# A hybrid decoder on one core: the first layer's W1 product in two column chunks as seven half-size products, x kept in memory meanwhile

## The chip, the cores and the metric

The kernel runs on one core of one Trainium2 chip. The metric is the time of one execution in device microseconds (us), the median of several runs; less is better. Engine names: PE is the matrix engine, DVE the vector engine, ACT the scalar engine, POOL the GpSimd engine, SP the engine that issues most transfers.

## What is computed

Two decoder layers on a sequence of 512 tokens with 1024 channels, everything in 32-bit floats. Each layer has a mixer (a windowed-mean mixer in the first layer, a gated spatial mixer, "SGU", in the second) and then an MLP; both are modulated by columns computed from a conditioning vector.

```
c_act = silu(c)
for i in range(2):
    sh1, sc1, g1, sh2, sc2, g2 = split(c_act @ ada_w[i] + ada_b[i], 6)
    h = rmsnorm(x, norm_mix_g[i]) * (1 + sc1) + sh1
    x = x + g1 * mixer_i(h)
    h = rmsnorm(x, norm_mlp_g[i]) * (1 + sc2) + sh2
    x = x + g2 * (square(relu(h @ mlp_w1[i])) @ mlp_w2[i])     # 1024 -> 4096 -> 1024
return rmsnorm(x, final_g)
```

## The kernel before

**Precision.** A 32-bit product is made from rounded parts. Each operand is split into a high part (a rounding copy on ACT, line 169 for weights, 594 for activations) and the rest (a subtraction on DVE, lines 170 and 595), and `mm3` (lines 176 to 182) issues three matmuls for one product: low by high, high by low, high by high. One split covers a weight block of 128 x 1024 in a buffer pair `wh`, `wl`; there are five such pairs.

**The MLP** is `mlp(i, ...)`, called once for each layer. The 4096 hidden columns come in four chunks of 1024. M1 is the product with W1, which gives one chunk of hidden values `g`; M2 multiplies a chunk by its 1024 rows of W2 and adds into `y`. The work is a list of units, written out by hand, which PE runs in that order:

- `f` units (`f_run`): an M1 product for 128 hidden columns, all 1024 input channels and all 512 tokens: 24 matmuls of width 512 in the first layer (`n = 256 if i else S`), 48 of width 256 in the second.
- `s` units (`s_run`): the seven half-size products of Strassen's scheme in Winograd's form for M1, for 512 hidden columns (a "quad" `(c, j)`): each has 24 matmuls of width 256. Seven `s` units do what four `f` units do. Their token-side sums (`as`, `sums_a`) are made once by `a_sums`; their weight-side sums are made in `s_prep`: two by a DVE addition (line 708), two by an accumulating transfer on POOL's queue (line 703).
- `p` units (`p_run`): the same scheme for M2 of chunks 0 to 2, seven units a chunk, 24 matmuls of width 512 each. `by_dma` (line 757) says how the weight-side sums are made. In the second layer POOL issues accumulating transfers of 1 MB into the tile `bt` (`b_add`, line 767): after the split for product 1 the block for product 5 is added, then the one for 6, then for 4, in this chain, and one more sum into a tile `b`. In the first layer DVE adds blocks that were loaded plainly (lines 783, 790, 806, 814).
- `q` units (`q_run`): M2 of chunk 3 done plainly, with the gated update of x (`gated`, lines 967 to 969) behind each.

In the first layer M1 consists of `f` units alone: seven column blocks of chunk 0 are computed in the "sweep" while the normalised input `hb` is made (lines 545 to 571), then 25 `f` units, 24 of them spread between the `p` units of the chunk before. In the second layer only chunk 0 is `f` units; chunks 1 to 3 are `s` units, two to three between any two `p` units. For each unit a `prep` function loads and splits its weights; `ahead` lets it run some units before the unit itself.

**What else fits between.** The modulation columns (`ada_tile`: a load of 512 KB and a DVE multiply-and-sum, line 202) are 128 channels each; 56 of them are computed in this manner behind the start: in the first layer's MLP 32, one every 0.69 unit (`due`); in SGU 24 (16 in its `u` loop, 8 in its output loop). `spread_cols` turns eight finished columns into the row tile `gb` with which `gated` multiplies: a transpose on PE, a copy on ACT, two transfers on POOL's queue.

**Room.** The token-side sums of the `s` units need two tiles of 1 MB. In the second layer they lie where x lay: `spill` writes x to memory, `reload` brings it back after the last `s` unit.

## Time and profile before

| | |
|---|---|
| three runs, median (range) | 866.25 us (865.43 to 867.08) |
| the profiled execution: time, span from first to last instruction | 867.54 us, 865.5 us |
| PE busy, weight loads busy | 850.8 us, 734.4 us |
| DVE busy, ACT busy, POOL busy | 667.8 us, 447.8 us, 49.4 us |
| granted PE clock | 0.998 |
| moved by DMA | 163.39 MB, mean 189 GB/s |

Busy times are unions of instruction records. A matmul's record is longer than the distance to the next one, since matmuls are pipelined: the distance between starts is what PE's time goes by. Line numbers are those of the kernel before. A group line of the profile gives line, engine, operation, out<-in tiles, shapes, count, then busy time, mean ns of one, and the engine's idle time before it with what ended it. "core N" windows give busy us (count) of PE, weight loads, DVE, ACT and POOL, then the clock, the DMA engines' mean busy share and GB/s.

### The profile page before, as it was taken

The page shows a single profiled execution, that of the slowest core. Times are in us where ns is not written, and L with a number is a line of the kernel's source. Part 1 is how long each engine was busy: PE and PEld are TensorE (multiplying, and loading weights), DVE is VectorE, ACT ScalarE, POOL GpSimd, SP SyncE. Part 2 cuts the span into 40 slices and gives each one's busy share as a digit, 9 for nine tenths or more (in the row PEclk, how much of TensorE's full clock was granted, in tenths as well). Part 3 has the DMA queues.
Part 4 walks back from the last instruction along what each step waited for, and adds up shares of the span by engine and source line. Part 5 has one row for each costly group of instructions (what it writes and reads, how often), then busy time and mean ns, then how long its engine had stood idle before and what let it go on. Part 6 is the DMA issues. An engine that isn't in the chain of part 4 may idle for free. (4 is left out here: it accounts for less than half of the span.)

```text
span 865.5 us, 11809 instructions
## 1 busy us (share of the span) xinstructions
PE 850.8 (98%) x4592; PEld 734.4 (85%) x4592; DVE 667.8 (77%) x884; ACT 447.8 (52%) x653; POOL 49.4 (6%) x69
## 2 busy tenths in 40 slices
PE   8999999999999999999999999999999999999996
PEld 7778888888888888888888888999999988999885
DVE  6889797788869886657798866667787598779855
ACT  5285755454444445238332326656765576567521
POOL 3000000000000000000020001001101000100001
PEclk9999999999999999999999999999999999999999
DMA  9969855453455341606757525946778587778302
GB/s 352 417 226 320 292 177 195 164 183 138 178 206 170 122 171 49 219 25 219 245 172 243 192 73 205 333 95 149 195 226 183 150 204 229 160 162 262 127 24 98
DMA packets 40045, 163.39 MB, mean 189 GB/s; under 512 B 4507, under 2 KB 4659, under 8 KB 34742
## 3 DMA queue, kind: packets, MB, share of 16 engines
q1 hardware_dynamic: 35282, 137.72, 44.4%
q0 software_dynamic: 4560, 24.66, 13.7%
q8 instruction: 36, 0.59, 0.3%
q10 hardware_dynamic: 148, 0.27, 0.1%
q14 instruction: 19, 0.16, 0.1%
HBM read 158.42 MB, written 4.21 MB: 188 GB/s over the span
## 5 line engine op out<-in xcount | busy, mean ns | idle before, releaser
L179 PE MATMUL po<-hb,wl 128*128 128x256 f32 (+1 forms) x624 | 207.7, 333 | 1.2 <-DVE wl L170 1.2
L180 PE MATMUL po<-hb,wh 128*128 128x256 f32 (+1 forms) x624 | 206.9, 332 | 0.2 <-DVE hb L595 0.2
L182 PE MATMUL po<-hb,wh 128*128 128x256 f32 (+1 forms) x624 | 206.7, 331 | 0.0
L170 DVE TENSOR_TENSOR wl<-raw,wh 128x1024 fp32r<-128x1024 f32 (+1 forms) x110 | 130.8, 1192 | 43.9 <-ACT wh L169 43.6
L169 ACT ACTIVATE wh<-raw 128x1024 fp32r<-128x1024 f32 (+1 forms) x110 | 113.1, 1034 | 67.3 <-PE pm L182 29.5
L182 PE MATMUL pm<-wh,oh 128*128 128x512 f32 x356 | 130.9, 377 | 0.0
L180 PE MATMUL pm<-wl,oh 128*128 128x512 f32 x336 | 130.8, 389 | 0.0
L179 PE MATMUL pm<-wh,ol 128*128 128x512 f32 x336 | 130.8, 389 | 0.0
L179 PEld LDWEIGHTS po<-hb,wl 128*128 128x128 f32 x624 | 117.2, 188 | 14.1 <-DVE wl L170 2.1
L180 PEld LDWEIGHTS po<-hb,wh 128*128 128x128 f32 x624 | 117.2, 188 | 12.0 <-DVE hb L595 0.4
L182 PEld LDWEIGHTS po<-hb,wh 128*128 128x128 f32 x624 | 117.1, 188 | 11.8
L170 DVE TENSOR_TENSOR wl<-b,wh 128x1024 fp32r<-128x1024 f32 x60 | 72.7, 1220 | 22.1 <-ACT wh L169 21.9
L202 DVE SCALAR_TENSOR_TENSOR ada<-ada,cb 128x1024 f32<-128x1024 f32 x56 | 68.1, 1218 | 19.4 <-DMA ada<-in_ada 19.1
L182 PEld LDWEIGHTS pm<-wh,oh 128*128 128x128 f32 x356 | 66.9, 188 | 13.9
L180 PEld LDWEIGHTS pm<-wl,oh 128*128 128x128 f32 x336 | 63.1, 188 | 12.4
L179 PEld LDWEIGHTS pm<-wh,ol 128*128 128x128 f32 x336 | 63.1, 188 | 12.4
L169 ACT ACTIVATE wh<-b 128x1024 fp32r<-128x1024 f32 x60 | 63.1, 1055 | 10.0 <-PE pm L182 6.5
L632 ACT ACTIVATE g<-po 128x512 f32<-128x512 f32 x40 | 23.6, 599 | 80.5 <-PE po L182 78.5
L170 DVE TENSOR_TENSOR wl<-bt,wh 128x1024 fp32r<-128x1024 f32 x24 | 29.0, 1222 | 35.0 <-ACT wh L169 35.0
L973 ACT ACTIVATE tmp<-x 128x512 f32<-128x512 f32 (+1 forms) x25 | 15.3, 612 | 63.3 <-DVE x L969 63.3
L862 DVE TENSOR_TENSOR y<-y,pm 128x512 f32<-128x512 f32 x68 | 43.5, 679 | 0.0
L179 PE MATMUL po<-as,wl 128*128 128x256 f32 x144 | 40.0, 278 | 0.9 <-DVE wl L170 0.9
(211 smaller groups left out, 1459.3 us busy)
## 6 DMA issues: line engine op xcount, KB each, us to landing
ada<-in_ada SPq DMA_DIRECT2D x72, 512.0 KB, 3.7
b<-in_w SPq DMA_DIRECT2D x21, 1024.0 KB, 5.2
raw<-in_w SPq DMA_DIRECT2D x25, 512.0 KB, 4.2
raw<-in_w1b SPq DMA_DIRECT2D x24, 512.0 KB, 6.3
bt<-in_w POOLq DMA_DIRECT2D x9, 1024.0 KB, 8.3
raw<-in_w2e SPq DMA_DIRECT2D x16, 512.0 KB, 3.2
raw<-in_w1b POOLq DMA_DIRECT2D x12, 512.0 KB, 5.4
wh<-in_ada SPq DMA_DIRECT2D x9, 512.0 KB, 9.6
```

Of the source, the lines that this page charges most:

```text
L169: A.activation(h[:, c], r[:, c], AF.Copy)
L170: V.tensor_tensor(l[:, c], r[:, c], f32(h[:, c]), ALU.subtract)
L179: T.matmul(o, wl, mh, start=first, stop=False, **kw)
L180: T.matmul(o, wh, ml, start=False, stop=False, **kw)
L182: T.matmul(o[:, c], wh, mh[:, c], start=False, stop=last and c.stop is None, **kw)
L202: V.scalar_tensor_tensor(r, r, 1.0, cb, ALU.mult, ALU.mult, accum_out=pmv[i, b][:, j : j + 1])
L632: A.activation(t, po, AF.Relu)
L862: V.tensor_tensor(yt, yt, banks[hf], ALU.subtract if minus else ALU.add)
L973: A.activation(tmp, xt, AF.Square, scale=D**-0.5, accum_out=s[:, len(cs) : len(cs) + 1])
```

## The change

- `FROM = (2, 1)`: the first layer's M1 for chunks 2 and 3 runs as 28 `s` units in place of 16 `f` units, in the order that the second layer has for chunks 1 to 3. W1's columns for them join the array `w1b`, indexed by `quad_at`.
- `a_parts` makes the token-side sums of the first layer from the split input (both parts subtracted, then added) in four steps, ahead of units 12, 13, 14 and 16.
- The first layer's nine remaining `f` units use width 256 too. The last matmul of a unit is cut in two (`narrow`, `two`) ahead of an `f` unit as well, and at the end of the sweep.
- x is written to memory from ACT's queue at the end of the sweep and brought back after the last `s` unit, as in the second layer.
- `by_dma = True`: the first layer's M2 sums too come from accumulating transfers on POOL's queue.
- The columns: 24 in the first layer's MLP at written-out units (`COLUMNS`: 12 of them at units 0 to 11, one at 18, 23, 28, 33, 38, 43 and 48 each into `gb`'s place, five at 58 to 61), 24 in SGU (19 in the `u` loop, 5 in the output loop), and 8 in the second layer's MLP, at units 8, 10, ... 22, into `gb`'s place. `spread_cols` for the MLP gains moves to unit 53 and to unit 30 of the second layer.
- `gb` is a tile of its own at each use; the input tile is placed anew ahead of the second layer's mixer.

```diff
+COLUMNS = (0, 1, 2, 3, 4, 5, 6, 7, 8, 9, 10, 11, 18, 23, 28, 33, 38, 43, 48, 58, 59, 60, 61, 61)
+A_PARTS = (12, 13, 14, 16)
...
+    def late_gb():
+        r = get_gb()
+        A.activation(r[:, 0:1], f32(latest[0])[:, 0:1], AF.Copy)
+        return r
...
+    def spill(h, queue=G):
+        xd.append(dram.tile([P, 2, D], F32, name=f"xd{h}{len(h32)}"))
+        queue.dma_start(xd[h], x_[h])
...
-                mm3(sweep[f], ((wh[:, fs[f]], wl[:, fs[f]])), (xh, xl), k == 0, k == KD - 1)
+                two = S // 2 if (k, f) == (KD - 1, SWEEP - 1) else None
+                mm3(sweep[f], ((wh[:, fs[f]], wl[:, fs[f]])), (xh, xl), k == 0, k == KD - 1, two)
+        for h in range(2):
+            spill(h, nc.scalar)
...
+    FROM = (2, 1)
...
-                n = 256 if i else S
+                n = 256
...
+            def a_parts(step):
+                blocks = [[H(slice(4 * j, 4 * j + 4), slice(256 * r, 256 * r + 256)) for j in range(2)] for r in range(2)]
...
+                def difference(p, q):
+                    t, u = scratch("s"), scratch("u")
+                    for n, o in enumerate((t, u)):
+                        V.tensor_tensor(o, f32(p[n]), f32(q[n]), ALU.subtract)
+                    V.tensor_tensor(t, t, u, ALU.add)
+                    return t
+                if step == 0:
+                    sums_a.update({1: blocks[0][0], 2: blocks[0][1], 4: blocks[1][1]})
+                    shift(hx, LINE - GAP)
+                    m, o = 5, operand(hx, "hx")
+                    sums_a["t"] = difference(blocks[1][0], blocks[1][1])
+                elif step < 3:
+                    m, o = (6, operand(big, "x0")) if step == 1 else (3, operand(big, "x1"))
+                    for q in range(2):
+                        V.tensor_tensor(sums_a["t"], sums_a["t"], f32(blocks[0][step - 1][q]), ALU.subtract if step == 1 else ALU.add)
+                else:
+                    m, o = 7, blocks[1][0]
+                    sums_a["t"] = difference(blocks[0][0], blocks[1][0])
+                parts(o, sums_a["t"] if step < 2 else sums_a.pop("t"))
+                sums_a[m] = o
...
-            by_dma = i == 1
+            by_dma = True
...
-                if i == 0:
+                if c + 1 < FROM[i]:
                     fs, lead, step = [("f", (c + 1, f)) for f in range(8)], 3, (1,) * 7
                 else:
                     fs, lead, step = [("s", (c + 1, j, m)) for j in range(2) for m in ORDER], 3, (2, 2, 2, 2, 2, 1, 0)
...
-                if i == 0:
+                if i == 0 and ("s", (FROM[0], 0, 1)) not in units[: n + 5]:
                     return min(n + 3, len(units))
...
+                if i == 0 and n in A_PARTS:
+                    a_parts(A_PARTS.index(n))
-                narrow[:] = [units[n + 1 : n + 2] and (units[n + 1][0] == "s" or i and units[n + 1] == ("q", (1, NT - 1)))]
+                narrow[:] = [units[n + 1 : n + 2] and (units[n + 1][0] in "sf" or i and units[n + 1] == ("q", (1, NT - 1)))]
...
-                if i and u == (3, 1, 4):
+                if u == (3, 1, 4):
                     reload()
...
+    ex = [(n, modulation(q, get_gb if 12 <= q < 19 else get4)) for q, n in enumerate(COLUMNS)]
+    ex.insert(19, (53, lambda: spread_cols(mods[0][:, c_g(1, 0) : c_g(1, 0) + KD], "gain0")))
+    mlp(0, first0, ex, gated, ending0)
...
+    ex = [(8 + 2 * q, modulation(48 + q, late_gb if q == 0 else get_gb)) for q in range(8)]
+    ex += [(30, lambda: spread_cols(mods[1][:, c_g(1, 0) : c_g(1, 0) + KD], "gain1"))]
+    mlp(1, first1, ex, last1, lambda: None)
...
+    w1b = np.concatenate([w1[0][:, 2 * D :], w1[1][:, D:]], axis=1)
+    d["w1b"] = w1b.reshape(2, 4, P, 10, 2, 256).transpose(3, 0, 4, 2, 1, 5).reshape(10, 2, 2, P, D)
```

The unit numbers of the first layer after the change: 0 the last `f` of chunk 0; 1 to 15 the eight `f` units of chunk 1 and the seven `p` of chunk 0; 16 to 36 the 14 `s` of chunk 2 and the seven `p` of chunk 1; 37 to 57 the 14 `s` of chunk 3 and the seven `p` of chunk 2; 58 to 65 the `q` units. In the second layer 0 to 3 are `f` units, and 4 to 24, 25 to 45 and 46 to 66 hold 14 `s` and seven `p` each.

More of the change, by code (lines that the diff above doesn't have):

```diff
@@ L941, in mlp @@
             ready = {}
-            extra = list(extra)
-            due, at = max(0.4, len(extra) / max(1, len(units) - 6)), 0
+            extra, at = list(extra), 0
             for n, (kind, u) in enumerate(units):
@@ L954, in mlp @@
                     a_sums(u[1] - 4)
-                if i and (kind, u) == ("p", (0, 1)):
-                    spread_cols(gain, "gain1")
-                if i and u == (3, 1, 4):
+                if u == (3, 1, 4):
                     reload()
@@ L1022, in first0, with modulation, ending0 @@
         return SWEEP
-    ex = [lambda q=q: ada_tile(0, 40 + q, ada1[q], get4) for q in range(8)]
-    ex += [lambda q=q: ada_tile(1, q, ada1[8 + q], get4) for q in range(24)]
-    ex.insert(12, lambda: spread_cols(mods[0][:, c_g(1, 0) : c_g(1, 0) + KD], "gain0"))
-    mlp(0, first0, ex, gated, lambda: normed(0, 1, 0))
+    def modulation(q, get):
+        return lambda: ada_tile(0 if q < 8 else 1, 40 + q if q < 8 else q - 8, ada1[q], get)
+    def ending0():
+        h_[0] = hparts(0)
+        normed(0, 1, 0)
+    ex = [(n, modulation(q, get_gb if 12 <= q < 19 else get4)) for q, n in enumerate(COLUMNS)]
+    ex.insert(19, (53, lambda: spread_cols(mods[0][:, c_g(1, 0) : c_g(1, 0) + KD], "gain0")))
+    mlp(0, first0, ex, gated, ending0)
     def blocks(src):
@@ L1076, in decoder_kernel @@
         u, gt, wu = {}, {}, {}
-        ex = [lambda: spread_cols(mods[1][:, c_g(0, 0) : c_g(0, 0) + KD], "gainm")]
-        ex += [lambda q=q: ada_tile(1, q, ada1[8 + q], get4) for q in range(24, 40)]
+        ex = [modulation(q, get4) for q in range(24, 32)]
+        ex += [lambda: spread_cols(mods[1][:, c_g(0, 0) : c_g(0, 0) + KD], "gainm")]
+        ex += [modulation(q, get4) for q in range(32, 43)]
         def do_u(n):
@@ L1111, in decoder_kernel @@
             (do_u if op[0] == "u" else do_mix)(int(op[1]))
-        ex += [lambda q=q: ada_tile(1, 40 + q, ada1[48 + q], get4) for q in range(8)]
+        ex += [modulation(q, get4) for q in range(43, 48)]
         h_[0] = hparts(GAP)
```

44 lines of the change are left out of this document (26 added, 18 removed).

## The prediction

> **What bounds the kernel now.** I read the page first: how much of the span PE is busy, and how busy its helpers are beside it.
>
> ```profile
> span 865.5 us, 11809 instructions
> PE 850.8 (98%) x4592; PEld 734.4 (85%) x4592; DVE 667.8 (77%) x884; ACT 447.8 (52%) x653; POOL 49.4 (6%) x69
> DVE  6889797788869886657798866667787598779855
> ```
>
> PE is busy 98% of the span, so only fewer or cheaper matmuls, or waits, can move the time. DVE at 77% is the second engine. In the waits of PE, almost nothing stands behind the start-up:
>
> ```profile
> PE po L179 <- DVE wl L170: 2.1, 4, 0.9
> ```
>
> Four times, 2.1 us in all, PE waited for the low part of a weight block. Next, PE's timeline tells what a unit costs. First a first-layer `f` unit (the start of one and of the next), then the second layer's `s` units (the first one, the next one, one that came late, and the end of the whole stretch).
>
> ```profile
> 267.14 0.39 PE L179 MATMUL po<-hb,wl 128*128 128x512 f32 x1
> ...
> 272.58 0.39 PE L179 MATMUL po<-hb,wl 128*128 128x512 f32 x1
> ```
>
> ```profile
> 583.50 0.28 PE L179 MATMUL po<-hb,wl 128*128 128x256 f32 x1
> ...
> 586.22 0.28 PE L179 MATMUL po<-as,wl 128*128 128x256 f32 x1
> ...
> 591.65 0.39 PE L179 MATMUL pm<-wh,ol 128*128 128x512 f32 x1
> ...
> 668.21 0.39 PE L179 MATMUL pm<-wh,ol 128*128 128x512 f32 x1
> ...
> 699.27 0.36 PE L179 MATMUL po<-as,wl 128*128 128x256 f32 x1 [0.86 <-DVE wl L170]
> ...
> 745.89 0.39 PE L179 MATMUL pm<-wh,ol 128*128 128x512 f32 x1
> ...
> 814.14 0.39 PE L179 MATMUL pm<-wh,ql 128*128 128x512 f32 x1
> ```
>
> An `f` unit takes 272.58 - 267.14 = 5.44 us for 24 matmuls, 0.2267 each at width 512. An `s` unit takes 586.22 - 583.50 = 2.72 us for 24, 0.1133 each at width 256: exactly half. The second layer's 42 `s` and 21 `p` units (24 matmuls of width 512 each, so 5.44) should take 42 x 2.72 + 21 x 5.44 = 228.5 us; they took 814.14 - 583.50 = 230.6. So the new arrangement of the first layer already runs in this trace, in the second layer, and loses 2.1 us over three chunks, of which about 1.0 is the one wait at 699.27 and the rest, 0.05 per `p`, the alternation of widths.
>
> **Matmuls.** Sixteen `f` units go: 16 x 5.44 = 87.04 us. Twenty-eight `s` units come: 28 x 2.72 = 76.16. That is **-10.9 us**, and all of it is on the path, since PE is. The nine other `f` units keep their time (48 x 0.1133 = 24 x 0.2267). Alternation: 21 `p` units at 0.05, **+1.0**.
>
> A rule speaks against this. The Trainium skill (TensorE: Matmul & The Clock Gate, Back-to-back issue gap) says that matmul spacing is set by weight load and matmul together and gives 81 ns at width 128 and 131 at 512, so that halving the width does not halve the spacing; estimated by a straight line, 98 ns at 256, the 28 units would cost 65.9 us against 50.3 for the 16. The trace disagrees: 0.1133 against 0.2267.
>
> **Work of DVE.** It is not on the path now; does it stay off? The rows of its pieces, and two starts that follow each other directly:
>
> ```profile
> L202 DVE SCALAR_TENSOR_TENSOR ada<-ada,cb 128x1024 f32<-128x1024 f32 x56 | 68.1, 1218 | 19.4 <-DMA ada<-in_ada 19.1
> L708 DVE TENSOR_TENSOR raw<-raw 128x1024 f32<-128x1024 f32 x12 | 14.6, 1220 | 0.1
> L783 DVE TENSOR_TENSOR b<-b 128x2048 f32<-128x2048 f32 x3 | 6.9, 2284 | 0.0
> L814 DVE TENSOR_TENSOR b<-b 128x2048 f32<-128x2048 f32 x3 | 6.8, 2281 | 0.0
> L747 DVE TENSOR_TENSOR g<-g,po 128x512 f32<-128x512 f32 x6 | 4.1, 680 | 0.3 <-PE po L182 0.3
> ```
>
> ```profile
> 156.99 1.22 DVE L170 TENSOR_TENSOR wl<-raw,wh 128x1024 fp32r<-128x1024 f32 x1
> 158.13 1.27 DVE L862 TENSOR_TENSOR y<-y,pm 128x512 f32<-128x512 f32 x2
> ```
>
> A piece of 1.22 us lets the next one start after 1.14. Removed: the four M2 additions (lines 783 to 814, of which the first and last are shown) x three chunks x 2.28 = 27.4 us, and eight columns, about 1.3 each with their small followers, 10.4. Added: 14 pieces of `a_parts` (4, 3, 3 and 4) x 1.14 = 16.0; two weight sums for each of four quads (line 708), 9.1; three additions from PSUM for each quad (line 747 and its like), 12 x 0.6 = 7.2; 12 more splits, 13.7. Net +8 us over 220. That is little, but it isn't spread evenly. The windows hold the first layer's chunk 1 stage and the second layer's first two:
>
> ```profile
> 186.00:262.00 76.00, 76.00 (x338) 62.81 (x337) 61.69 (x71) 35.29 (x45) 1.28 (x2) 1.00 0.47 169
> 668.00:746.00 78.00, 77.14 (x516) 70.56 (x515) 61.63 (x64) 47.26 (x57) 6.81 (x8) 1.00 0.74 190
> 583.00:668.00 85.00, 85.00 (x589) 78.62 (x589) 65.77 (x62) 57.94 (x75) 8.79 (x11) 1.00 0.72 184
> ```
>
> The row 668 to 746 has the very units that the first layer will have as 16 to 36: DVE 61.6 us. There, the last step of `a_parts` (4 x 1.14 = 4.6) and four columns (5.2) come on top: 71.4 us in 7 x 5.44 + 14 x 2.72 = 76.2, or 94%. The first three steps of `a_parts` (11.4) lie at units 12 to 14, where the additions that go (two of 2.28 there) and lead make room; the sums are wanted only from unit 17 on, so I cost them at nothing, and at their full 11.4 if that room isn't there. In the second layer's first chunk the eight columns raise 65.8 to 76 of 85 us. ACT, at 47 of 78 us, has room.
>
> **The chain of accumulating transfers.** The sums for M2 products 1, 5, 6 form a chain: split, transfer, split, transfer, split. The first layer has no such chain now and gets three. POOL's timeline shows the first and third link of each of the second layer's three chains, and the line's own view the time to landing:
>
> ```profile
> 586.80 0.85 POOL L767 DMA_DIRECT2D bt<-in_w  x1 [9.97 <-DVE wl L170]
> ...
> 612.23 0.88 POOL L767 DMA_DIRECT2D bt<-in_w  x1 [2.76 <-DVE wl L170]
> ...
> 664.10 0.85 POOL L767 DMA_DIRECT2D bt<-in_w  x1 [2.02 <-DVE wl L170]
> ...
> 691.81 0.85 POOL L767 DMA_DIRECT2D bt<-in_w  x1 [13.26 <-DVE wl L170]
> ...
> 742.38 0.85 POOL L767 DMA_DIRECT2D bt<-in_w  x1 [2.62 <-DVE wl L170]
> ...
> 768.20 0.86 POOL L767 DMA_DIRECT2D bt<-in_w  x1 [13.04 <-DVE wl L170]
> ```
>
> ```profile
> DMA to landing us min/median/max: 7.8/8.4/9.8
> ```
>
> PE goes from product 1 to product 6 in 2 x (5.44 + 2 x 2.72) = 21.8 us. The chain took 25.4, 27.7 and 25.8: it slips by 3.7, 5.9 and 4.1. What it may slip is its lead, the first link's issue ahead of product 1 on PE (591.65, 668.21, 745.89): 4.9, 4.1 and 3.5. Only the second overran clearly (by 1.8), and it is the one with the wait at 699.27: while ACT and DVE stand at the split that needs the transfer, the splits of the `s` units queue behind it. So an overrun costs its size less about 0.7, and no chain has anything to spare. What I expect: first layer, chunk 0: the cover is the lead there (p1's split ends some 10 us early, below), so 0. Chunk 1: slip 4.6 (the mean) and one column, 1.3, is 5.9; a lead of 4.2 less some 1.3 for the crowded DVE is 2.9; 3.0 over, costs 2.3. Chunk 2: slip 5.9 with a column, lead 4.2, costs 1.0. Second layer, chunk 0, with three columns on the chain: slip 3.7 + 3.9, lead 4.9, costs 2.0 if all of them fall on it, 0 if they fill DVE's idle time; I take 1.0. Together **+4.3** (0 to 10).
>
> The Trainium skill (DMA: Bandwidth & Descriptors, Measured) has 6.15 us for a 1 MB transfer issued from GpSimd. By that, an estimate, each link would be over 2 us shorter, no chain would slip, and the sum would be lower by the whole 4.3. The trace's 8.4, for accumulating ones among other traffic, decides.
>
> **Writing x out.** Two transfers of 1 MB from ACT's queue, with nothing to wait for, start about 92 us, among the loads for the first units.
>
> ```profile
> 100.00:104.00 4.00, 4.00 (x19) 3.32 (x18) 1.20 (x2) 4.00 (x8) 0.00 (x0) 1.00 0.98 352
> ```
>
> ```profile
> 104.77 1.22 DVE L170 TENSOR_TENSOR wl<-raw,wh 128x1024 fp32r<-128x1024 f32 x1
> ```
>
> ```profile
> 114.67 0.39 PE L179 MATMUL po<-hb,wl 128*128 128x512 f32 x1
> ```
>
> The DMA engines are full there (0.98, 352 GB/s), so 2 MB delay the loads by 2.1/0.352 = 6 us. The split that ends at 106.0 is wanted at 114.67: 8.7 us of lead cover it. I cost it at nothing; twice the delay would cost 3. Bringing x back happens as in the second layer, where nothing waited.
>
> **SGU.** Three fewer columns in its output loop, three more in its `u` loop. At the end of that loop a column lies ahead of the input's low parts, and PE waits right after:
>
> ```profile
> 531.79 1.22 DVE L202 SCALAR_TENSOR_TENSOR ada<-ada,cb 128x1024 f32<-128x1024 f32 x1
> ```
>
> ```profile
> 535.89 0.38 PE L179 MATMUL po<-hb,wl 128*128 128x256 f32 x1 [0.22 <-DVE wl L170]
> ```
>
> Gone, it gives at most its 1.14 us; against a possible loss of as much in the `u` loop I take **-0.5** (-1.1 to +1.1). The moved `spread_cols` have two POOL transfers each, and whatever accumulating transfer is queued behind the second waits for the first to land. At unit 53 no such transfer follows but x's return; at unit 30 of the second layer the next in line is the sum for product 4, wanted 20 us later. Nothing.
>
> **Sum.** -10.9 + 1.0 + 4.3 - 0.5 = -6.1 us. The profiled execution took 867.5 (span 865.5 and 2.0 around it), so 861.4 for its like; it lies 1.3 above the median of 866.25, for which the sum gives **860.2**.
>
> **Rivals.** *DVE becomes the bound (slower).* In 668 to 746 DVE idles 78.0 - 61.6 = 16.4 us, partly because it stands in order behind ACT's wait for the transfers. If this idle time cannot be filled by the added 9.8 us, units 16 to 36 take 71.4 + 16.4 = 87.8 instead of 76.2: 11.6 lost there, and 1.0 each in the two other chains. -10.9 + 1.0 + 13.6 - 0.5 = +3.2: 869.5. It decides as soon as all waits together pass 10.4. For it: 94%, five buffer pairs, and the second layer lost only 1.0 at 79%. Against: columns and `a_parts` hang on no transfer and can lie in just that idle time.
>
> *The waits don't come.* The columns fill the gaps, the chains hold: -10.9 + 1.0 + 0 - 0.5 = -10.4: 855.9. For it: two of three chains lost nothing. Against: their lead is used up.
>
> *Half the width isn't half the time.* With the first layer's `s` units on the weight load instead (734.4/4592 = 0.160 us each by the page), they would take 28 x 24 x 0.160 = 107.5, +20.5 with the rest of the sum as it is: 891. Against: 0.1133 in the second layer, same operands, same shapes. The skill's rule above is this case.
>
> **How the numbers follow.** Forecast (waits between 1 and 8 us) 0.62; no waits 0.19; DVE the bound or waits above 8: 0.17; half width dear 0.02. A measurement of this kernel can tell about 0.2%, 1.7 us, from no change. Faster: the forecast, the second rival and none of the others, less a little at the upper edge, 0.80; waits of 8.7 to 12.1 are within 0.2%, 0.07; slower 0.13. The range goes from 855.5 (no waits) to 865.0 (waits of 9.1) and leaves out about 0.17, nearly all above.
>
> **What would show it.** Matmuls of width 256 on `as` and `hb` in the first layer at 0.1133 apart, and M1 and M2 there (units 0 to 57) shorter by 5 to 11 us: the first term. PE waits on "DVE wl" or on ACT behind `bt`, near products 5 and 6 of chunks 1 and 2 and in the second layer's first chunk: the third. DVE above 90% in units 16 to 36 with waits below 3 us would refute the first rival. I am wrong if PE's waits in the first layer sum to over 8 us, if the first units wait for loads that x's way out delays, or if the `s` units' spacing isn't 0.1133.

## The result and the profile after

| | median of the runs (range) | against before in the same job |
|---|---|---|
| before | 865.84 us (864.63 to 867.08) | |
| changed | 898.69 us (898.25 to 899.08) | 1.0379 times [1.0361, 1.0397] |

The forecast was 860.2, 855.5 to 865.0. The page of the changed kernel, the lines that answer to those of before:

```profile
span 896.5 us, 13013 instructions
PE 857.0 (96%) x5116; PEld 758.1 (85%) x5116; DVE 685.5 (76%) x918; ACT 467.8 (52%) x682; POOL 66.7 (7%) x91
DVE  6889466897898688677798856666788698779855
PEclk9999999998999999999999999999999999999999
```

PE is down from 98% to 96% of a longer span: it stood for 39.5 us where it stood for 14.7 before, 24.8 more. DVE is no busier by share than before. The tenth slice (202 to 224 us) shows a lower granted clock, which before had nowhere. To see where the time went, the run is cut at starts of matmuls. The first layer's M1 and M2 run from the first of these rows of PE's timeline to the second:

```profile
122.62 0.39 PE L186 MATMUL pm<-wh,ol 128*128 128x512 f32 x1
...
364.11 0.39 PE L186 MATMUL pm<-wh,ql 128*128 128x512 f32 x1
```

That is 241.5 us. The same cut in every profiled execution, in us ("layer 1" and "layer 2" are these M1/M2 stages; "q", the plain product for chunk 3, follows layer 1; "M1, chunk 0" is what lies between SGU and layer 2's first M2 product):

| kernel | start | layer 1 | q | SGU | M1, chunk 0 | layer 2 | end | span |
|---|---|---|---|---|---|---|---|---|
| before | 120.1 | 228.6 | 45.3 | 141.9 | 55.8 | 222.5 | 51.4 | 865.5 |
| changed | 122.6 | 241.5 | 45.3 | 146.8 | 55.8 | 232.8 | 51.6 | 896.5 |
| E1 no column transfers | 121.9 | 227.3 | 45.3 | 141.9 | 53.8 | 224.2 | 51.8 | 866.2 |
| E2 M2's sums by DVE | 121.2 | 230.1 | 45.7 | 147.1 | 53.6 | 233.9 | 51.6 | 883.2 |
| E3 x written out later | 122.6 | 242.3 | 45.7 | 144.6 | 56.0 | 234.3 | 51.7 | 897.0 |
| E4 before, M2's sums by transfers | 119.6 | 245.7 | 45.3 | 141.9 | 54.7 | 223.3 | 51.2 | 881.8 |
| E6 E4 without column transfers | 119.5 | 228.6 | 45.3 | 141.5 | 55.1 | 222.0 | 51.5 | 863.5 |
| E10 E1 without `a_parts`' sums | 121.8 | 223.2 | 45.3 | 142.2 | 53.6 | 223.5 | 51.9 | 861.6 |
| E11 eight columns moved to SGU | 121.3 | 245.6 | 46.0 | 143.7 | 54.2 | 222.2 | 51.9 | 884.8 |
| E13 columns paced, waited for | 121.2 | 244.4 | 45.8 | 144.7 | 53.6 | 234.9 | 51.7 | 896.2 |
| E18 columns paced, not waited for | 121.6 | 236.5 | 45.3 | 151.0 | 54.4 | 225.5 | 51.7 | 886.0 |

The 31 us are layer 1 (+12.9), layer 2 (+10.3), SGU (+4.9) and the start (+2.5). Most of the start's 2.5 is no wait: from 60 to 100 us the 512-wide matmuls follow each other at 0.233 us in the changed kernel and in every one built from it, at 0.227 in before, E4 and E6; 167 of them make 1.1 us. In the changed kernel the 194 of width 256 behind them are 0.1177 apart, not 0.1133, which makes another 0.9. No run tests the reason; that the place of buffers can do such a thing is seen in E17 below.

Layer 1 was to be 228.6 - 10.9 + 1.0 = 218.7 us without waits, so it lost 22.8. What PE waited for in it (columns: total us, times, longest):

```profile
PE po L186 <- DVE wl L177: 5.0, 4, 2.1
PE pm L187 <- DVE wl L177: 5.0, 2, 3.4
PE po L186 <- ACT g L810: 3.7, 1, 3.7
PE pm L186 <- DVE ol L621: 1.2, 1, 1.2
```

Together 14.9 us, where before has no PE wait in this stage. All lie before 230 us, while M2 works on chunk 0 and the first units of chunk 1, but for one of 0.26 us. They are mostly waits for low parts of weight blocks (`wl`, 10.0 us). What holds DVE up is in the groups of its instructions, here of the whole span; the row that answers to line 202 is

```profile
L209 DVE SCALAR_TENSOR_TENSOR ada<-ada,cb 128x1024 f32<-128x1024 f32 x56 | 68.3, 1221 | 53.7 <-DMA ada<-in_ada 53.4
```

The same 56 column instructions as before, as long as before, but DVE stood 53.4 us ahead of them for their transfers, not 19.1; in layer 1 it is 21.2 us, against 8.6. The columns' time from issue to landing between 100 and 345 us, before and then changed:

```profile
DMA to landing us min/median/max: 3.1/3.3/5.0
```

```profile
DMA to landing us min/median/max: 3.4/5.2/11.7
```

The longest such wait of DVE, in DVE's and ACT's timelines (start, duration, and in brackets the idle time before it and its releaser):

```profile
121.95 1.22 DVE L858 TENSOR_TENSOR s<-s,g 128x1024 f32<-128x1024 f32 x1
131.46 1.23 DVE L209 SCALAR_TENSOR_TENSOR ada<-ada,cb 128x1024 f32<-128x1024 f32 x1 [8.29 <-DMA ada<-in_ada]
132.61 0.08 DVE L209 DVE_READ_ACCUMULATOR ada<-ada,cb 128x1 f32 x1
132.61 1.22 DVE L177 TENSOR_TENSOR wl<-bt,wh 128x1024 fp32r<-128x1024 f32 x1
```

```profile
130.74 1.06 ACT L176 ACTIVATE wh<-bt 128x1024 fp32r<-128x1024 f32 x1 [10.62 <-DMA bt<-in_w]
```

For 8 us of chunk 0 DVE stands at a column and ACT at the tile of the chain, both for transfers that are under way together. The DMA view of 113 to 133 us shows what is on the way, with each queue's packets, MB and share of the 16 engines:

```profile
DMA packets 1076, 4.96 MB, mean 248 GB/s; under 512 B 128, under 2 KB 128, under 8 KB 818
q0 software_dynamic: 288, 2.10, 53.7%
q1 hardware_dynamic: 786, 2.83, 38.4%
ada<-in_ada SPq DMA_DIRECT2D x3, 512.0 KB, 11.2
b<-in_w POOLq DMA_DIRECT2D x1, 1024.0 KB, 10.4
bt<-in_w POOLq DMA_DIRECT2D x1, 1024.0 KB, 14.1
```

Two accumulating transfers (last column: us to landing) took 10.4 and 14.1, where the forecast had 8.4 from the second layer, and three columns took a median of 11.2. The DMA engines are 92% busy (53.7 and 38.4) and move only 248 GB/s.

### The profile page after: what moved, and what is told of

Its sections match the earlier page's. It is cut to its first block, busy times and chain, and to the rows that moved or that the text cites. A ratio compares the mean times of both kernels' runs of the same rounds, so it can differ in the third digit from the quotient of the medians.

```text
span 896.5 us, 13013 instructions
## 1 busy us (share of the span) xinstructions
PE 857.0 (96%) x5116; PEld 758.1 (85%) x5116; DVE 685.5 (76%) x918; ACT 467.8 (52%) x682; POOL 66.7 (7%) x91
## 3 DMA queue, kind: packets, MB, share of 16 engines
q1 hardware_dynamic: 35282, 137.72, 41.9%
q0 software_dynamic: 7728, 43.53, 23.9%
## 5 line engine op out<-in xcount | busy, mean ns | idle before, releaser
L177 DVE TENSOR_TENSOR wl<-raw,wh 128x1024 fp32r<-128x1024 f32 (+1 forms) x122 | 145.4, 1195 | 32.7 <-ACT wh L176 32.5
L176 ACT ACTIVATE wh<-raw 128x1024 fp32r<-128x1024 f32 (+1 forms) x122 | 125.5, 1034 | 76.9 <-DVE raw L774 22.5
L186 PEld LDWEIGHTS po<-hb,wl 128*128 128x128 f32 x696 | 131.4, 189 | 9.4 <-DVE wl L177 3.1
L187 PEld LDWEIGHTS po<-hb,wh 128*128 128x128 f32 x696 | 132.0, 190 | 4.6 <-DVE hb L621 0.4
L189 PEld LDWEIGHTS po<-hb,wh 128*128 128x128 f32 x697 | 131.9, 189 | 4.3
L189 PE MATMUL pm<-wh,oh 128*128 128x512 f32 (+1 forms) x375 | 131.2, 367 | 0.0
L209 DVE SCALAR_TENSOR_TENSOR ada<-ada,cb 128x1024 f32<-128x1024 f32 x56 | 68.3, 1221 | 53.7 <-DMA ada<-in_ada 53.4
L177 DVE TENSOR_TENSOR wl<-bt,wh 128x1024 fp32r<-128x1024 f32 x48 | 57.8, 1222 | 45.0 <-ACT wh L176 45.0
L186 PE MATMUL po<-as,wl 128*128 128x256 f32 x240 | 69.1, 288 | 13.6 <-ACT g L810 8.2
L176 ACT ACTIVATE wh<-bt 128x1024 fp32r<-128x1024 f32 x48 | 49.5, 1052 | 61.0 <-DMA bt<-in_w 54.7
L189 PE MATMUL po<-as,wh 128*128 128x256 f32 x240 | 68.3, 285 | 0.0
L187 PE MATMUL po<-as,wh 128*128 128x256 f32 x240 | 68.3, 285 | 0.0
L186 PEld LDWEIGHTS po<-as,wl 128*128 128x128 f32 x240 | 47.0, 196 | 14.9 <-ACT g L810 8.6
```

Source lines behind the costliest of these rows:

```text
L176: A.activation(h[:, c], r[:, c], AF.Copy)
L177: V.tensor_tensor(l[:, c], r[:, c], f32(h[:, c]), ALU.subtract)
L186: T.matmul(o, wl, mh, start=first, stop=False, **kw)
L187: T.matmul(o, wh, ml, start=False, stop=False, **kw)
L189: T.matmul(o[:, c], wh, mh[:, c], start=False, stop=last and c.stop is None, **kw)
L209: V.scalar_tensor_tensor(r, r, 1.0, cb, ALU.mult, ALU.mult, accum_out=pmv[i, b][:, j : j + 1])
```

## The experiments

The quoted texts say VectorE for DVE, ScalarE for ACT and SyncE for SP, and name the theories: **A**, DVE stands in its fixed order at columns whose transfers land late beside accumulating transfers, and the splits behind it come late; **B**, the chains of accumulating transfers are too long by themselves, or DVE too full; **C**, x's way out delays the loads of the first units; **E**, `a_parts` finds no room on DVE; later **D**, not DVE's wait but the column transfers themselves crowd the DMA engines, whoever waits. **F**, named in one text, puts a wait down to ACT's own order. Where the first texts give 241 us for the second layer, they count from its first `s` unit, some 8 us ahead of the table's cut. Ratios are to before, in the same job.

**E1, no column transfers** (869.03 us, 1.0019 [1.0004, 1.0033]):

```diff
-        nc.sync.dma_start(r, src)
...
-        V.scalar_tensor_tensor(r, r, 1.0, cb, ...)
+        V.scalar_tensor_tensor(r, cb, 1.0, cb, ...)
```

> The changed kernel with the transfers of the 56 modulation columns left out (the DVE instruction reads the row tile twice instead, so its time stays; what the columns contain is therefore not computed). Theory A (DVE stands in its fixed order at a column whose transfer has not landed, 53.4 us of such idle time in the changed kernel): nearly all of the new waits go; the first layer's M1/M2 stage falls from 241.5 us to 219 to 224, the second layer's from 241.2 to 231 to 233, the total from 898.7 to 866 to 873. Theory B (the chains of accumulating transfers are too long and DVE too full): the stages keep most of their waits, 235 or more and 237 or more, total 888 to 896. Theory C (writing x out is what floods the transfers): the second layer's stage keeps its 241, the first loses a few us at most.

**E2, M2's sums in the first layer by DVE again** (885.08, 1.0206 [1.0174, 1.0239]):

```diff
-            by_dma = True
+            by_dma = i == 1
```

> The changed kernel with the first layer's M2 sums made by DVE again. Theory A: the accumulating transfers (10 to 14 us to landing in the first layer, two engines' time per byte) are what delays the columns there, so the first layer's M1/M2 stage falls from 241.5 us by 8 or more, though DVE has 27 us more to do; the second layer keeps its 241. Total 884 to 891. Theory B, DVE part: the 27 us of DVE work come on top of a full engine and the stage gets longer, total 900 to 912. Theory B, chain part: the stage falls to about 222, total 880.

**E3, x written out at unit 6** (899.24, 1.0356 [1.0324, 1.0388]), not at the sweep's end:

```diff
-        for h in range(2):
-            spill(h, nc.scalar)
...
+                if i == 0 and n == 6:
+                    for h in range(2):
+                        spill(h, nc.scalar)
```

> The changed kernel with x written to memory at unit 6 of the first layer instead of at the end of the sweep. Theory C (its 2 MB, out between 90 and 101 us, make the loads, the first accumulations and the first columns late): start and first chunk lose 5 to 8 us less, total 890 to 894. Theories A and B: the 2 MB collide with the second link of the chain instead; total within 3 us of 898.7.

**E4, the kernel before with M2's sums by transfers and nothing else** (881.78, 1.0171 [1.0117, 1.0226]):

```diff
-            by_dma = i == 1
+            by_dma = True
```

> The kernel before with only one part of the change: the first layer's M2 sums by accumulating transfers, M1 and the columns as they were. Theory A: the columns come at 0.69 a unit and from three buffers, so only a few arrive late: 866 to 870. Theory B: three chains with links of 12 to 14 us against a pace of 10.9: 3 to 6 us each, 875 to 884.

E1 takes 30 of the 31 us away, though layer 1, at 227.3, stays above the 219 to 224 of theory A. E3 takes nothing, so C falls. E2 repairs layer 1 alone (230.1). In E4 one line alone costs layer 1 17.1 us, more than the net 12.9 of the whole change. That is what B's text gave, and A's 866 to 870 is missed; but E4's column row shows 89.4 us of waiting (19.1 before):

```profile
L202 DVE SCALAR_TENSOR_TENSOR ada<-ada,cb 128x1024 f32<-128x1024 f32 x56 | 68.2, 1221 | 89.5 <-DMA ada<-in_ada 89.4
```

**E6, E4 without column transfers** (865.26, 0.9983 [0.9971, 0.9995]): E4's and E1's edits together, on before.

> The kernel before with the first layer's M2 sums by accumulating transfers, and the column transfers left out (the columns' values are not computed). Theory A: the stage that was 245.7 us with the columns (228.6 before) comes back to 228 to 231, total 864 to 868. Theory B (the three chains by themselves): it stays at 238 or more, total 874 or more.

Layer 1 is back at 228.6 us. So accumulating transfers alone cost layer 1 nothing, which B can't explain, columns alone (before) cost nothing, and both together cost 17.

**E5, columns used later** (898.63, 1.036 [1.0332, 1.0388]): in the MLPs a column is loaded at one unit and used one to three units later; in SGU 16 columns lie in the `u` loop and 8 behind it.

```diff
+        return [(at, 1, load), (at + lag, 0, lambda: ada_use(i, t, held[0]))] if lag else [(at, 1, modulation(q, get))]
...
-        ex += [modulation(q, get4) for q in range(32, 43)]
+        ex += [modulation(q, get4) for q in range(32, 40)]
```

> The changed kernel, with the same column transfers and the same DVE instructions, but each column used one unit (first eleven), three units (units 18 to 48) or two units (second layer, loads three units apart) after its load was issued; in SGU, 17 of the pops again in the u loop and eight columns in the output loop. If DVE standing in order at columns that haven't landed is the cause (theory A): first layer's M1/M2 stage from 241.5 us to 229 to 235, SGU from 146.8 to 142 to 144, second layer's stage from 232.8 to 224 to 227, total 876 to 886. If the DMA engines as such are too full (theory D: bytes, not order), nothing is gained by using them later: 893 or more.

A miss: DVE's instructions are put in order by a scheduler, not as written, and the trace shows the lag gone and 40.2 us of waits still at the 26 columns that were to be used later. SGU's part worked: 142.2 us.

**E7, E1 with `a_parts` spread** (869.99, 1.0029 [1.0014, 1.0044]), and **E8, E5, E2 and E7's list together** (882.34, 1.0169 [1.0134, 1.0204]):

```diff
-A_PARTS = (12, 13, 14, 16)
+A_PARTS = (12, 14, 16, 18)
```

> The changed kernel without the column transfers (their values are not computed) and with the four steps of the token-side sums ahead of units 12, 14, 16 and 18 instead of 12, 13, 14 and 16. Theory E (the 8.6 us that the first layer's stage still loses without column transfers come from ACT and DVE standing at these sums, above all the one wait of 4.9 us at 193.8): stage from 227.3 to 220 to 224, total 860 to 865. Theory B: the chain and the full DVE lose it wherever the sums lie: 226 to 229, total within 2 us of 869.

> The changed kernel with the columns used later and SGU's split as in the first of these runs, the first layer's M2 sums by DVE, and the token-side sums ahead of units 12, 14, 16 and 18. Theories A and E: the stage that took 230.1 us with DVE's sums alone falls to 222 to 227, SGU 142 to 144, the second layer 224 to 227; total 863 to 872. If DVE is simply full there (238.8 of 250 us by the sum of its pieces): stage 230 or more, total 872 to 880.

E7 has layer 1 at 229.4, where E's text had 220 to 224, a miss: moving `a_parts` by a unit or two does nothing. E8 is a miss too. It is E2 with SGU at 143.7; layer 1 stays at 230.1 us, of which DVE is busy 220.4 in E2, and layer 2 at 234.7.

**E9, columns transferred but not waited for** (903.21, 1.0421 [1.0398, 1.0444]):

```diff
-        V.scalar_tensor_tensor(r, r, 1.0, cb, ALU.mult, ALU.mult, ...)
+        V.scalar_tensor_tensor(cb, cb, 1.0, cb, ALU.mult, ALU.max, ...)
```

> The changed kernel with all 48 column transfers in their places, but VectorE's column instruction takes the resident row of c twice instead of the landed column (the modulation values are not computed from the columns), so it waits for no transfer. Theory A, what costs is that VectorE stands in its fixed order until a column has landed: the first layer's M1/M2 stage falls from 241.5 to 227 to 231 us, the second layer's from 232.8 to 224 to 227, the gating unit from 146.8 to 142, the median to 867 to 874 us, as when the transfers are left out. Rival theory D, what costs is the bytes (the columns' 512 KB each fill the DMA engines, or hold the slots of the raw tiles, so that weight blocks and the chains' tiles come late whoever waits): the first layer's stage stays at 238 us or more and the median at 885 or more. A time between the two gives each its share: the part above 869 is the bytes'.

SGU (141.8) and layer 2 (226.0) did what A says; layer 1 grew to 255.7, which A excludes and D's "238 us or more" admits without explaining the growth. Two things had moved. Freed of their waits, the transfers bunched at the start of the stage; and the scheduler put column instructions of later stages into it: DVE is busy 222.2 us in layer 1, against 193.6. The run doesn't decide.

**E10, E1 without the ten subtractions and additions of `a_parts`** (864.13, 0.9961 [0.9943, 0.9979]). The lines show one of its three places.

```diff
...
-                        V.tensor_tensor(o, f32(p[n]), f32(q[n]), ALU.subtract)
-                    V.tensor_tensor(t, t, u, ALU.add)
-                    return t
+                    return f32(p[0])
```

> The changed kernel without the column transfers (as in the run that had them left out) and without the ten subtractions and additions of blocks of x's parts ahead of M1's chunk (each about 1.1 to 1.2 us on VectorE; the operands are then copies of plain blocks, so M1's sums are not the right ones). Theory E, the 8.6 us that the first layer's stage keeps above 218.7 us without the columns come from VectorE having no room in units 12 to 18 for these instructions: the wait of 4.9 us near 194 us goes, the stage falls from 227.3 to 219 to 223 us, the median from 869.0 to 861 to 865. Rival theory F, the wait comes from ScalarE's own order (the copy out of M1's first bank queued behind the halves of M2's tiles, which wait for transfers): the wait stays, the stage at 226 or more, the median at 867 to 869.

In E1 one wait of PE, 4.65 us at 198.68, is most of what layer 1 keeps; in E10 it is gone, and 4.1 us of the stage with it (3.3 us of other waits stand in E10). The timeline of E1, then the windows of E1 and E10 (busy us and count of PE, weight loads, DVE, ACT and POOL, then clock, DMA, GB/s): DVE is full in E1 and not in E10.

```profile
198.68 0.58 PE L186 MATMUL po<-as,wl 128*128 128x256 f32 x1 [4.65 <-ACT g L809]
```

```profile
186.00:199.00 13.00, 8.34 (x60) 7.59 (x60) 12.97 (x14) 7.94 (x11) 1.71 (x2) 0.96 0.84 175
```

```profile
186.00:199.00 13.00, 13.00 (x96) 12.21 (x95) 11.16 (x10) 8.91 (x12) 1.71 (x2) 1.00 0.74 132
```

PE waits there for a copy out of PSUM on ACT (`g`, L809), which queues behind a split that waits for a weight-side sum of DVE. So E holds and F doesn't, for about half of the 8.6 us by which E1 exceeded 218.7; the other half stays open.

**E11, the second layer's eight columns moved into SGU** (885.9, 1.0219 [1.0191, 1.0248]): two beside each group of the first product there, sixteen in the `u` loop, eight behind.

```diff
+                for q in range(24 + 2 * (2 * ch + hf), 26 + 2 * (2 * ch + hf)):
+                    modulation(q, get4)()
...
-        ex += [modulation(q, get4) for q in range(32, 43)]
+        ex += [modulation(q, get4) for q in range(32, 48)]
...
-        ex += [modulation(q, get4) for q in range(43, 48)]
+        ex += [modulation(q, get_gb if 0 else get4) for q in range(48, 56)]
```

> The changed kernel with the second layer's eight columns taken out of its M1/M2 stage and put into the gating unit: eight columns beside the first product there (two to each group of banks), sixteen in the middle product's, eight in the last's. Nothing of the first layer is touched. Theory A: the second layer's stage falls from 232.8 to 223 to 225 us, the gating unit from 146.8 to 142 to 144 (no accumulating transfer runs there, so columns land in about 4.2 us), the first layer's stays at 241 to 243, the median comes to 884 to 888. Rival, 32 columns are too many for the gating unit's VectorE: that stage gets longer than 147 us and the median is 889 or more.

Layer 2 falls from 232.8 to 222.2 and SGU from 146.8 to 143.7, with 32 columns where 24 were. Layer 1 wasn't touched and yet came out at 245.6, above the 241 to 243 of the text: a few us between two profiled executions carry little there.

**E12 and E13, a pair**: each column's transfer in the MLPs waits for one element that ScalarE writes into its tile; E12 has E9's edit too (893.3, 1.0294 [1.0261, 1.0327]), E13 waits for the columns (899.14, 1.0361 [1.0328, 1.0395]).

```diff
+            if q < 24 or q > 48:
+                A.activation(r[:, 0:1], f32(latest[0])[:, 0:1], AF.Copy)
```

> All 48 column transfers, again with VectorE's column instruction reading only the resident row of c, so that it waits for none of them (the values are not computed from the columns); but each column's transfer in the M1/M2 stages must first wait for ScalarE to write one element of its tile out of the weight tile split last, so that SyncE can't issue the columns in a bunch at the stage's start, as it did when they were merely not waited for (255.7 us for the first layer's stage). Its partner is the same kernel with the wait left in. Theory A (VectorE standing in its order): the first layer's stage comes to 227 to 232 us, 8 or more below the partner's, the median to 867 to 874. Theory D (the transfers' load on the DMA engines, whoever waits): the first layer's stage stays at 238 or more, within 3 us of the partner's.

> The changed kernel with the pacing alone: each column's transfer in the M1/M2 stages first waits for one element that ScalarE writes out of the weight tile split last; VectorE reads the columns and waits for them as in the changed kernel, and the results are its. Both theories: the first layer's stage near the changed kernel's 241.5 us (238 to 246; a transfer that starts later is waited for longer, but the bunch of columns before the stage is spread), the second layer's near 232.8, the gating unit 146.8, the median 893 to 905.

Layer 1: 245.9 and 244.4. That would refute A, but E12 has 222.3 us of DVE work in the stage and E13 196.3: again later columns' instructions had come in.

**E14, E15, E16**: the column's instruction writes the tile first, and its transfer comes behind: of 512 KB (895.78, 1.0332 [1.0284, 1.038]), 256 KB (888.38, 1.0265 [1.0238, 1.0292]) or 32 KB (880.61, 1.0171 [1.0152, 1.0191]).

```diff
-        nc.sync.dma_start(r, src)
...
-        V.scalar_tensor_tensor(r, r, 1.0, cb, ...)
+        V.scalar_tensor_tensor(r, cb, 1.0, cb, ...)
+        nc.sync.dma_start(r, src)    # E15: r[:, 0:S], E16: r[:, 0:64]
```

> The changed kernel with the two steps of a column exchanged: VectorE's instruction writes the tile from the resident row of c (the values are not computed from the columns), and the column's 512 KB are transferred into the tile behind it. So VectorE does the same instructions in nearly the same places, it waits for no column, and each transfer still starts at its place in the stage. Theory D (the bytes, beside the accumulating transfers): the first layer's M1/M2 stage stays at 238 to 246 us and the median at 888 or more, less what the gating unit and the second layer gain. Theory A (VectorE's standing): the stage comes to 227 to 231, the median to 867 to 873.

> The same with half of each column's bytes (256 KB). Theory D: the first layer's stage lies between the whole transfers' and 227.3, near 232 to 237. Theory A: 227 to 231 again.

> The same with a sixteenth of each column's bytes (32 KB): the control for what SyncE's transfers waiting behind VectorE's instructions cost by themselves. Both theories: the first layer's stage near the 227.3 us of the run without column transfers (226 to 230), the median 867 to 872. If it stays above 235, SyncE's queue standing behind VectorE is what these three runs measure, and they decide nothing.

Layer 1: 244.0, 244.4 and 235.3 us. The last is just over the 235 at which the text says that they decide nothing, and the reason shows in its trace: a column's instruction waits for its slot, and so for the landing of the column before. That takes up to 10.0 us even for 32 KB:

```profile
DMA to landing us min/median/max: 1.7/2.9/10.0
```

**E17 and E18**: E12, with the instruction held in its place by one element per partition that ScalarE copies from a weight tile. E17 (895.99, 1.0335 [1.031, 1.036]) keeps it in a small new tile, E18 (889.69, 1.0259 [1.0235, 1.0282]) in a pad tile that takes room already; the lines are E18's.

```diff
+        pin = pins[:, pinned[0] : pinned[0] + 1]
+        A.activation(pin, f32(latest[0])[:, 0:1] if latest[0] is not None else vec[:, 0:1], AF.Copy)
...
+        V.scalar_tensor_tensor(cb, cb, pin, cb, ALU.mult, ALU.max, ...)
```

> The paced kernel (each column's transfer in the M1/M2 stages behind one element that ScalarE writes out of the weight tile split last) with VectorE's column instruction held in its place by one element per partition, which ScalarE copies from the same weight tile, and reading only the resident row of c beside it: it waits for its place, but for no transfer (the values are not computed from the columns). The transfers on SyncE and the instructions on VectorE stand in nearly the order of the paced kernel that does wait, whose first layer's stage was 244.4 us. Theory A (VectorE's standing): the stage comes to 227 to 232 us, the second layer's to 224 to 227, the median to 867 to 875. Theory D (the transfers beside the accumulating ones, whoever waits): the stage stays at 238 to 246 us, the median at 882 or more.

> The run before again (columns paced, VectorE's column instruction held in its place by an element from ScalarE and waiting for no transfer), but with those elements in a pad tile that the kernel has anyway, so that no buffer behind them moves in on-chip memory. In the run before, the 512-wide matmuls followed each other at 233.8 ns from the first layer's M1/M2 stage to the end, against 227.4 in every other kernel, and the 256-wide ones at 117.3 against 114; the stage was 235.9 us. Expected of the moved buffers: the spacing is back at 227.4 and 114 ns. Theory A (VectorE's standing): the first layer's stage comes to 227 to 231 us against the partner's 244.4, the waits between its first sixteen units stay gone, the second layer's stage comes to 223 to 228, the median to 868 to 878. Theory D (the transfers themselves): the stage stays at 238 or more.

In E17 every unit of layer 1 is 3% longer, which is the new tile's doing (last section). E18 against E13 is the cleanest pair: nearly the same order on DVE, the same bytes, DVE as busy in layer 1 (194.6 us against 196.3), and no wait of it for a column, where E13 has 7.2 us of them. Layer 1 falls from 244.4 to 236.5 and layer 2 from 234.9 to 225.5, and the ratios to before (1.0361 and 1.0259) are 9 us of the whole time apart; both A's range for layer 1 (227 to 231) and D's (238 or more) are missed, while layer 2 is as A had it. (SGU's 151.0 holds one wait of PE of 6.9 us behind the held instructions themselves.) What PE still waits for in E18's layer 1:

```profile
PE po L188 <- DVE wl L179: 7.0, 5, 2.7
PE po L188 <- ACT g L815: 2.5, 1, 2.5
PE pm L189 <- DVE wl L179: 2.3, 4, 0.8
```

And what ACT waits for there: `bt` tiles, nearly as long as in the changed kernel (E18's waits first, then the changed kernel's row of who waited for the chain's transfers: total us and times from 90 us to the stage's end).

```profile
ACT wh L178 <- DMA bt<-in_w: 35.1, 6, 9.3
```

```profile
  ACT wh L176: 36.5, 6
```

That last wait isn't what E18 keeps over E1, where ACT stands 34.1 us at `bt` too. What E18 has and E1 has not is 11.2 us of ACT standing at plainly loaded weight tiles (`raw`); the longest, 7.3 us, ended at 157.83 with a load issued at 147.71.

**What follows.** That the two kinds of transfers together make the loss is shown (before, E4 and E6). Who passes it on to PE is shown in part. In the second layer A accounts for nearly all: 9.4 of the 10.7 us by which E13 exceeds E1. In the first layer it accounts for 7.9 of 17.1; the other 9.2 stay although DVE waits for no column, and go when the transfers go (E1). E13 says so too: its DVE stands 7.2 us at columns in layer 1, not 21.2, yet the stage is no shorter than the changed kernel's. Which of the late landings makes the 9.2 isn't settled. The crowded DMA engines (D) are the likeliest, since plain weight loads land late. But E18's extra copies on ACT are not excluded, nor is SyncE's queue, which in E18 stands 54.2 us at columns for those copies, with weight loads queued behind. With no column transferred at all the changed kernel is at 1.0019, so making the transfers land earlier can't by itself beat before; E10 and E6, which are below 1, leave out work that is wanted.

## Why the prediction failed, step by step

**Matmuls, -10.9: right.** An `s` unit on `as` and the next on `hb`, in the first layer:

```profile
300.70 0.29 PE L186 MATMUL po<-as,wl 128*128 128x256 f32 x1
...
303.44 0.28 PE L186 MATMUL po<-hb,wl 128*128 128x256 f32 x1
...
306.15 0.39 PE L186 MATMUL pm<-wh,ol 128*128 128x512 f32 x1
```

2.74 and 2.71 us. The rival on half width is out. The stage would be 218.7 us by these terms; E10 comes to 223.2.

**The chains, +4.3: the step that failed.** Of it 3.3 us were for layer 1, which lost 22.8; E4 and E6 put 17.1 us on chains and columns together and none on the chains alone. The step went through the chains one by one with landing times of 7.8 to 9.8 us, measured in a stage of before with no column in it, and counted each column only as 1.3 us of DVE, with no wait for its transfer. The sentence "chunk 0: the cover is the lead there (...), so 0" was the worst: that is where a dozen columns' transfers (units 0 to 11) meet the chain, and where a good half of the stage's PE waits lie. I had listed what is queued behind the chain's waits, but not asked what the chain's transfers do to the other transfers. The chains of chunk 2 did hold. The criterion "PE's waits in the first layer sum to over 8 us" was met with 14.9. (With each link 2.25 us shorter, as the aside has it, the second chain would still have slipped by 5.9 - 4.5 = 1.4 us, inside its lead; the sum doesn't change.)

**Second layer, +1.0: mis-sized**, measured 10.3. Its columns, 1.3 us of DVE each in the sum, kept DVE standing 12.1 us at their transfers; PE's waits, in layer 2:

```profile
PE po L186 <- ACT g L810: 4.5, 1, 4.5
PE po L186 <- DVE wl L177: 3.4, 2, 2.8
PE po L186 <- DVE g L817: 0.5, 1, 0.5
```

**SGU, -0.5: wrong sign**, measured +4.9. Three more columns at the end of the `u` loop delay the low parts of the gated tiles: PE waited 2.5 us for `gtl`, and its clock fell after. The possible loss there, put at as much as one column's 1.14, had no row behind it. E1 (no transfers) and E5 (16 columns in the loop) both give 142.

**`a_parts`, "at nothing, and at their full 11.4 if that room isn't there":** the room was not there; E10 gives 4.1 without columns.

**x's way out, nothing: right as far as E3 goes**, which moves it and has the same start of 122.6. **Not in the sum:** the spacing of 0.233 in the start, some 2 us. The prediction took every matmul's spacing from before. **The rival that DVE becomes the bound** had the right engine for `a_parts`' place, but the rest of its mechanism was not this: DVE is 80% busy in layer 1 (193.6 of 241.5 us) and stands still, waiting. Its time, 869.5, is nearly 30 us short too: of the branches it is "waits above 8", at 0.17 with this one, that came.

## What to carry to other kernels

A transfer's time to landing, read in one stage, holds for the traffic of that stage only: before moving work from an engine to transfers, add up for the new stage the time that all transfers together take of the DMA engines. An instruction that is off the critical path but waits for a load stands in the queue ahead of those that are on it; when loads get slower, it is that queue which shows it. And an experiment that removes a wait may set a scheduler free to move work: compare the orders and the busy times before believing it.

## What the runs showed of the hardware

**An accumulating byte costs the DMA engines about twice as much.** Queue lines of the page, before and then changed (packets, MB, share of 16 engines over the span):

```profile
q1 hardware_dynamic: 35282, 137.72, 44.4%
q0 software_dynamic: 4560, 24.66, 13.7%
```

```profile
q1 hardware_dynamic: 35282, 137.72, 41.9%
q0 software_dynamic: 7728, 43.53, 23.9%
```

The change puts 18.9 MB on POOL's queue and takes none off the other. At 0.239 x 896.5 / 43.53 = 4.9 us per MB, against 0.419 x 896.5 / 137.72 = 2.7 on the queue of plain loads, that is 93 us of all engines. That it is the adding and not the queue is seen in before: a plain transfer of 1 MB on POOL's queue (x's way out, 524.8 to 529.0 us), then a link of the chain (586.8 to 595.1), with the same packets and bytes:

```profile
q0 software_dynamic: 144, 1.05, 60.8%
```

```profile
q0 software_dynamic: 144, 1.05, 69.5%
```

The first is 0.608 x 4.2 = 2.6 us of all engines, the second 0.695 x 8.3 = 5.8. The Trainium skill (Collectives: The Full Stack, The bandwidth ceiling: the fold count and why AG ≠ RS ≠ AR) says of collectives that a reducing transfer costs more because it reads two sources and not one. These figures agree with that in size; no run here shows the reads apart.

**After some waits the matmuls run at half speed for a while.** Behind the wait of 3.7 us for `g`, in the changed kernel:

```profile
211.39 0.58 PE L186 MATMUL po<-as,wl 128*128 128x256 f32 x1 [3.70 <-ACT g L810]
211.77 0.41 PE L187 MATMUL po<-as,wh 128*128 128x256 f32 x1
211.98 0.41 PE L189 MATMUL po<-as,wh 128*128 128x256 f32 x1
```

```profile
211.20:216.50 5.30, 5.11 (x24) 5.11 (x25) 5.30 (x6) 3.58 (x5) 1.25 (x2) 0.50 0.98 198
```

Spacing 0.213 us where 0.1133 is usual, and a granted clock of 0.50 (the window's third number from the end). 44 matmuls of width 256 in layer 1, nearly all behind two waits, were over 0.2 us apart, which is 4.6 us on top of the 14.9 of waits. So a wait can cost more than its length. It need not be long, nor does the slow stretch start at its end:

```profile
141.46 0.38 PE L186 MATMUL po<-hb,wl 128*128 128x256 f32 x1 [2.05 <-DVE wl L177]
...
142.41 0.42 PE L187 MATMUL po<-hb,wh 128*128 128x256 f32 x1
142.63 0.41 PE L189 MATMUL po<-hb,wh 128*128 128x256 f32 x1
```

Nor does every wait bring it: behind one of 3.36 us, which ended at 168.05, the clock stayed at 1.00.

```profile
168.00:174.00 6.00, 5.95 (x42) 5.53 (x43) 5.90 (x10) 0.00 (x0) 0.00 (x0) 1.00 0.90 334
```

The Trainium skill (TensorE: Matmul & The Clock Gate, Part 1: The HAM clock gate) has a gate that halves the clock after an idle window of about 3.4 us. The half speed agrees; the length doesn't, since a wait of 2.05 us was enough here and one of 3.36 was not.

**With buffers moved, matmuls were slower.** E17's new tile shifts what lies behind it, and little else sets it apart from E18; an M2 product took 137.85 - 132.24 = 5.61 us, and 5.46 in E18, where the elements lie in the pad:

```profile
132.24 0.39 PE L186 MATMUL pm<-wh,ol 128*128 128x512 f32 x1
...
137.85 0.28 PE L186 MATMUL po<-hb,wl 128*128 128x256 f32 x1
```

```profile
132.54 0.39 PE L188 MATMUL pm<-wh,ol 128*128 128x512 f32 x1
...
138.00 0.29 PE L188 MATMUL po<-hb,wl 128*128 128x256 f32 x1
```

The usual distance of 512-wide matmuls is 0.2338 us in layers 1 and 2 of E17 and 0.227 in E18's; in SGU (420 to 500 us) it is 0.2267 in both, so not every matmul is touched. How the place does it no run shows.
